# Split weights at shifted addresses in the gate and up stage, and a norm factor spread through DRAM

## The chip, the cores and the metric

The kernel runs on one core of a Trainium2 chip. The metric is the device time of one execution in microseconds. Before the change it was 1467.61 us, the median of three runs (1467.38, 1467.61 and 1486.37 us).

## The reference, cut to what matters

The program is one decoder block on 256 tokens of width 2048, in float32. Two token mixers run on the normed input, an attention and a gated DeltaNet; their outputs are raised to width 2048, gated and added. Then come the output projection and the feed-forward part, which the change touches:

```python
x = x + mixed @ w_o[l]
h2 = rms_norm(x, norm2_w[l])
x = x + (jax.nn.silu(h2 @ w_ffn_gate[l]) * (h2 @ w_ffn_up[l])) @ w_ffn_down[l]
return rms_norm(x, norm_f_w)
```

`rms_norm` multiplies each token's row by one factor, 1/sqrt(mean of squares + eps), and by a weight for each column. The hidden width of the feed-forward part, `D_FF`, is 5632.

## The kernel before, in words

**Matmuls in three parts.** The weights come from DRAM as float32 in pieces of 128 x 2048 words (1 MB, `load`, L134, issued by SP). Each half of a piece is split into a rounded high part `hi` (ScalarE, L159) and the rest `lo` (VectorE, L160), by `split`. There are three `hi` and three `lo` buffers of 1024 words a partition, used in turn. The activations are kept in the same two parts, and a product is three matmuls: high by high, high by low, low by high.

**Two forms of matmul loop.** `group_t` (L234) holds the split weights still: a block of 128 x 128 of `hi` or `lo` is loaded into TensorE, and 256 columns of the activations stream through it. One call makes 256 output features for all tokens. A half of a piece gives 24 such matmuls (16 from `hi`, 8 from `lo`), a call with two pieces 96. `group` and `pair` (through `nat_mm`, L260 to L262) do it the other way: 128 x 128 of the activations stand still, and 512, 354 or 356 columns of the split weights stream.

**Stages in order of time.** The first projection (three blocks 354 and 356 wide, "zab") runs from the start; then `wdn`, `nsa` and `wmg`, 36 calls of `group_t` with the activations `hh`, one `group` ("nsav") between them, and the mixers' own small matmuls put in between by `pump`, which after each half of a piece advances generators that were queued with `add`. Then 16 short calls for `wud` and `wun` (activations `odn` and `onsa`), 48 matmuls each; four `group` calls for `wo` with activations `xa`; 44 calls for gate and up with activations `h2` (named `h` in the profile); and four `group` calls for `wd` with activations `fa` and `fxy`.

**Gate and up.** The loop runs over 22 groups `g`; each makes a gate call and an up call, 192 matmuls together, 4224 in all. After the gate call VectorE multiplies by the factor of norm 2 (`R2b`, L1244), ScalarE takes SiLU (L1245), GpSimd multiplies by the factor again (L1246); after the up call VectorE multiplies the two (L1248) and the product is split into `fa`.

**The factor of norm 2.** VectorE makes two numbers per partition, `r2` (L1213, and `rsqrt`, L275 to L279). Every partition needs all 256 of them in a row: `row_bcast` (L1062) multiplies with the identity on TensorE, once for each half of the tokens, and VectorE copies the result out (L1066). The generator `bcast2` puts the two matmuls after the third and the fourth half of the first gate call.

**The kick.** Before `wud`, a generator `kick` (L965) puts four transposes of the identity, whose result nobody reads, after the first half.

**What sets the order.** Tile's scheduler places instructions per engine in program order, with `split` raised in priority, so that the splits run ahead of their matmuls. Instructions under `pin` keep their order.

**Addresses.** As the program is laid out, the `hi` buffers begin at bytes 41088, 45184 and 49280 of each partition, the `lo` buffers at 53376, 57472 and 61568, the activations `hh` at 78144, `odn` at 127552, `onsa` at 111168, `h2` at 177728, and `xa` and the first `fa` at 78208. The blocks inside them step by 512 or 1024 bytes. So in all `group_t` calls the standing operand begins 64 bytes after the streaming one, counted modulo 256. In `nsav` the same difference is 192, in `wo` it is 0, and so it is in `wd`.

Of the kernel before, what the change touches and what calls it, by code (L numbers as in the profile page):

```python
# [7 lines left out]
F32 = mybir.dt.float32  # L8
F32R = mybir.dt.float32r
# [5 lines left out]
P = 128  # L15
# [3 lines left out]
DFF = 5632  # L19
NFG = DFF // 512  # L20
EPS = 1e-6
ZW = 4288

XW = (4144, 4112, ZW)
NEG = -1e30
# [70 lines left out]
class Kern:  # L96
# [40 lines left out]
    def split_one(self, rv, w, h, ahead):  # L137

        nc = self.nc
        hi = self.wp.tile([P, 1024], F32R, tag="hi", bufs=self.NH, name=self.nm("hi"))  # L140
        lo = self.wp.tile([P, 1024], F32R, tag="lo", bufs=self.NH, name=self.nm("lo"))
        hv = hi[:, :2 * w].rearrange("p (k n) -> p k n", n=w)
        lv = lo[:, :2 * w].rearrange("p (k n) -> p k n", n=w)
        with self.tc.high_priority(offset=self.HP):
            for k in range(2):
                self.pin(nc.scalar.activation(hv[:, k, :], rv[:, 2 * h + k, :], AF.Copy))  # L146
                ahead(2 * h + k)
                self.pin(nc.vector.tensor_tensor(lv[:, k, :], rv[:, 2 * h + k, :], hv[:, k, :].bitcast(F32), op=OP.subtract))
        return hv, lv

    def split(self, rv, w, h):
        nc = self.nc
        m = rv.shape[1] // 2
        hi = self.wp.tile([P, 1024], F32R, tag="hi", bufs=self.NH, name=self.nm("hi"))
        lo = self.wp.tile([P, 1024], F32R, tag="lo", bufs=self.NH, name=self.nm("lo"))
        hv = hi[:, :m * w].rearrange("p (k n) -> p k n", n=w)
        lv = lo[:, :m * w].rearrange("p (k n) -> p k n", n=w)
        with self.tc.high_priority(offset=self.HP):
            nc.scalar.activation(hv, rv[:, m * h:m * h + m, :], AF.Copy)  # L159
            nc.vector.tensor_tensor(lv, rv[:, m * h:m * h + m, :], hv.bitcast(F32), op=OP.subtract)  # L160
        return hv, lv
# [244 lines left out]
    def prep_k(self, pre, cT, hg):  # L406
# [15 lines left out]

        V.tensor_scalar(ss[:], ss[:], EPS, None, op0=OP.add)
        rk = self.rsqrt(ss[:], [2, 4], "rk")
# [99 lines left out]
    def prep_q(self, pre, cT, hg):  # L524
# [5 lines left out]
        for t in range(2):  # L530
# [7 lines left out]
            sq.free()  # L538
        V.tensor_scalar(ss[:], ss[:], EPS, None, op0=OP.add)
        rq = self.rsqrt(ss[:], [2, 4], "rq")  # L540
# [135 lines left out]
    def dn_norm(self, o, t, hg):  # L676
# [9 lines left out]
        V.scalar_tensor_tensor(ss[:], ss[:], 1.0 / 128, cq, op0=OP.mult, op1=OP.mult)  # L686
        V.tensor_scalar(ss[:], ss[:], EPS, None, op0=OP.add)
        r = self.rsqrt(ss[:], [4], "ro")
# [35 lines left out]
    def nsa_kv(self):  # L724
# [3 lines left out]

        while not self.ar.idle("z", ZW):
            yield  # L730
        self.ar.drop("z", ZW)
        zt = self.xy.tile([P, ZW], F32R, tag="z", name="zkh")
        KH = zt[:, 0:2176].rearrange("p (k n) -> p k n", k=2)
# [224 lines left out]
        for v in self.vn:  # L958
            v.free()

    def kick(self):

        bv = self.v4(self.aux("kick"))
        for j in range(4):
            self.pin(self.nc.tensor.transpose(bv[:, j, :], self.cs["ident"], self.cs["ident"]))  # L965
        yield


    def build(self):
        ctx, tc, nc, t = self.ctx, self.tc, self.nc, self.t  # L970
        V = nc.vector
        self.NH = 3
        self.HP = 600
        self.wp = ctx.enter_context(tc.tile_pool(name="wp", bufs=3))
        self.cp = ctx.enter_context(tc.tile_pool(name="cp", bufs=1))
# [32 lines left out]
        self.ar.add("y", ys, 4096)  # L1008
        zs_ = self.xy.tile([P, ZW], F32, tag="z", name="zsg")
        ws_ = self.xy.tile([P, 4096], F32, tag="w", name="wsg")  # L1010
        self.ar.add("z", zs_, ZW)
        self.ar.add("w", ws_, 4096)
# [39 lines left out]
        def norm_factor(ss, name):  # L1052
            v = self.small([2], name + "v")
            V.tensor_scalar(v[:], ss, 1.0 / D, EPS, op0=OP.mult, op1=OP.add)
            r = self.rsqrt(v[:], [2], name)
            return r

        def row_bcast(r, name, steps=1):

            bank = self.aux(name)  # L1060
            for tt in range(2):
                self.pin(nc.tensor.matmul(bank[:, tt * P:(tt + 1) * P], r[:, tt:tt + 1].to_broadcast([P, P]), self.cs["ident"], start=True, stop=True))  # L1062
                if tt == 0 and steps == 2:
                    yield
            R = self.cp.tile([P, 256], F32, name=name)
            V.tensor_copy(R[:], bank[:, :256])  # L1066
            return R
# [5 lines left out]
        rstd1 = self.small([2], "rstd1")  # L1073

        def evac_zab(g, ps):
            w = ZAB_W[g]
            o = 40 if g == 0 else 0
            z0 = sum(ZAB_W[:g]) + o - 40
            for tt in range(2):
                if g == 0:  # L1080
                    V.tensor_scalar(ab[:, tt, :], ps[tt][:, 0:16], rstd1[:, tt:tt + 1], None, op0=OP.mult)
                    V.tensor_scalar(self.gat[:, tt, :], ps[tt][:, 16:40], rstd1[:, tt:tt + 1], None, op0=OP.mult)
                nc.scalar.activation(self.zs[:, tt, z0:z0 + w - o], ps[tt][:, o:w], AF.Silu, scale=rstd1[:, tt:tt + 1])
# [19 lines left out]
        def rms1(ps):  # L1103
            ss = self.small([2], "ssx1")
            V.tensor_reduce(ss[:], ssx[:], axis=AX.X, op=OP.add)
            v = norm_factor(ss[:], "r1")
            V.tensor_copy(rstd1[:], v[:])
            xT.free()
            xn.free()
            evac_zab(0, ps[0])  # L1110
            yield
            evac_zab(1, ps[1])
            yield
            self.R = yield from row_bcast(rstd1, "R1")
            yield from self.dn_small(ab)

        zab = [[t[f"zab{g}"][c] for c in range(4)] for g in range(3)]
        self.add(rows_in())
        ps = self.pair(zab[:2], hact, ZAB_W, first)
        self.add(rms1(ps))  # L1120
        ps = self.group(zab[2], hact, ZAB_W[2])
        evac_zab(2, ps)
# [36 lines left out]
        for g in range(16):  # L1159
            e = self.group_t([t["wmg"][g * 2 + c] for c in range(2)], hact)  # L1160
            m = self.ar.alloc([2, 256])
# [4 lines left out]

        dact = lambda k: self.odn[:, :, k, :]
        nact = lambda k: self.onsa[:, :, k, :]
        self.add(self.kick())
        for g in range(8):  # L1170
            for m in (mg[g], mg[8 + g]):
                self.pin(nc.scalar.activation(m.ap, m.ap, AF.Sigmoid))
# [4 lines left out]
        for g in range(8):  # L1177
            e = self.group_t([t["wun"][g]], nact)
            m = mg[8 + g]
# [18 lines left out]
        for g in range(4):  # L1198
            ps = self.group([t["wo"][g * 4 + c] for c in range(4)], mact)
            cs = slice(g * 512, g * 512 + 512)  # L1200
            for tt in range(2):
# [4 lines left out]
                bv = self.v4(bank)  # L1206
# [6 lines left out]
        V.tensor_reduce(sst[:], ss2[:], axis=AX.X, op=OP.add)  # L1213
        r2 = norm_factor(sst[:], "r2")

        def bcast2():
            for _ in range(2):
                yield
            R2 = yield from row_bcast(r2, "R2", 2)
            self.R2b = R2[:, None, :].to_broadcast([P, 2, 256])  # L1220

        self.add(bcast2())
        h2 = lambda k: hh[k // 4][:, :, k % 4, :]


        fa = []
        for g in range(2 * NFG):
            i = g // 2
            if g % 2 == 0:
                if i < 4:  # L1230
                    if i == 0:
                        fh = self.four(self.hp, "a", "fa", 16, 16)
                    f = fh[i]
                elif i < 10:
                    if i % 2 == 0:
                        j = i // 2 - 2
                        xyt = self.xy.tile([P, XW[j]], F32R, tag="xyz"[j], name=f"fxy{i}")[:, 16 * (j == 1):][:, :4096].rearrange("p (a k n) -> p a k n", a=4, k=4)
                    f = xyt[:, i % 2 * 2:i % 2 * 2 + 2]
                else:
                    f = pb.tile([P, 2064], F32R, name=f"fa{i}")[:, 16:].rearrange("p (l k n) -> p l k n", l=2, k=4)  # L1240
                fa.append(f)
            e = self.group_t([t["wfg"][g * 4 + c] for c in range(2)], h2)
            sgt = pb.tile([P, 2, 256], F32, tag="tmp", bufs=4, name=self.nm("sgt"))
            V.tensor_tensor(sgt[:], e, self.R2b, op=OP.mult)  # L1244
            nc.scalar.activation(sgt[:], sgt[:], AF.Silu)  # L1245
            nc.gpsimd.tensor_tensor(sgt[:], sgt[:], self.R2b, op=OP.mult)  # L1246
            e = self.group_t([t["wfg"][g * 4 + 2 + c] for c in range(2)], h2)
            V.tensor_tensor(sgt[:], e, sgt[:], op=OP.mult)  # L1248
            self.hilo(fa[i][:, :, g % 2 * 2:g % 2 * 2 + 2, :], sgt[:])
        fact = lambda k: fa[k // 4][:, :, k % 4, :]  # L1250
        w_ = pb.tile([P, 4 * 2048 + 48], F32, tag="h2", name="wf")[:, 0:D]
        nc.scalar.dma_start(w_, t["wf"])
# [15 lines left out]
        for g in range(4):  # L1268
# [4 lines left out]
            for tt in range(2):  # L1273
# [8 lines left out]
                if g == 3:  # L1282

                    root = self.small([1], f"root{tt}")
                    nc.scalar.activation(root[:], part, AF.Sqrt, bias=sv)
                V.tensor_scalar(sv, part, sv if g else EPS, None, op0=OP.add)
                if g < 3:
# [110 lines left out]
```

## Time and profile before

| | before |
|---|---|
| median of three runs | 1467.61 us |
| the profiled execution's own time | 1468.2 us |
| its span | 1466.4 us |
| TensorE busy with matmuls | 1453.2 us, 99% |
| VectorE busy | 901.9 us, 62% |
| ScalarE busy | 687.7 us, 47% |
| GpSimd busy | 78.9 us, 5% |
| mean granted clock of TensorE | 0.998 |

The span runs from the first to the last instruction; the profiled execution's own time is 1.8 us more. A matmul's duration in the profile overlaps the next one's, so the pace of a row of matmuls is read from the starts of its first and last, or from a stretch's length and the number of matmuls in it. A stretch's count takes in a matmul that began before it and still ran.

### The profile page before, as it was taken

To read this page: it belongs to the slowest core of one execution; us is meant where nothing else is said; L and a number is where in the kernel's file an instruction comes from. 1 tells how busy PE (TensorE), PEld (TensorE's weight loads), DVE (VectorE), ACT (ScalarE), POOL (GpSimd) and SP (SyncE) were. 2 spreads that over 40 slices of the span, in tenths; PEclk is the share of its full clock that TensorE was granted. 3 is DMA by queue.
4 is the path that set the end of the run, shared out by engine and by line. 5 is a ranking of instruction groups with operands and counts; after the bars stand their busy time and mean duration, and the time that the engine had idled before them with its cause. 6 is when DMAs were issued, how large, how long until landed. Compare 5 with 4: busy or idle time off the path is not lost.

```text
span 1466.4 us, 26003 instructions
## 1 busy us (share of the span) xinstructions
PE 1453.2 (99%) x11021; PEld 1387.7 (95%) x11021; DVE 901.9 (62%) x1352; ACT 687.7 (47%) x850; POOL 78.9 (5%) x69
## 2 busy tenths in 40 slices
PE   9999999999999999999999999999999999999997
PEld 8999999999999999998899999999999998888886
DVE  6678998667687755566565555555555554545454
ACT  5655444354455545444454444444444444444343
POOL 1000101000000000120000000000000000000000
PEclk9999999999999999999999999999999999999999
DMA  8754546435554455555555555555555556555553
GB/s 334 244 201 173 176 162 223 138 129 198 202 198 151 139 204 183 185 180 195 177 197 189 189 198 201 183 194 199 200 187 190 200 198 208 197 200 185 192 198 115
DMA packets 41541, 279.20 MB, mean 190 GB/s; under 512 B 5056, under 2 KB 5584, under 8 KB 9552
## 3 DMA queue, kind: packets, MB, share of 16 engines
q1 hardware_dynamic: 38880, 270.08, 52.7%
q10 hardware_dynamic: 1440, 4.82, 0.9%
q0 software_dynamic: 1104, 2.64, 0.6%
q8 instruction: 86, 1.41, 0.4%
q14 instruction: 31, 0.25, 0.0%
HBM read 274.62 MB, written 2.89 MB: 189 GB/s over the span
## 4 chain that ended last, share of the span: by engine, by line
PE 97%; DMA 1%; DVE 1%; ACT 0%; issue 0%; SPq 0%; DVEq 0%; ACTq 0%
PE mm L234 65%; PE mm L261 9%; PE mm L262 9%; PE mm L260 9%; DMA raw<-in_zab 1%; PE oacc L919 1%; PE U L589 1%; DVE lo L160 0%; PE pt L905 0%; PE hid L772 0%; PE x1T L1208 0%; PE hid L773 0%; ACT hi L159 0%; PE o L606 0%; PE vn L606 0%; PE P L573 0%
## 5 line engine op out<-in xcount | busy, mean ns | idle before, releaser
L160 DVE TENSOR_TENSOR lo<-raw,hi 128x1024 fp32r<-128x1024 f32 (+2 forms) x510 | 617.4, 1212 | 430.5 <-ACT hi L159 429.7
L159 ACT ACTIVATE hi<-raw 128x1024 fp32r<-128x1024 f32 (+2 forms) x510 | 533.6, 1049 | 639.3 <-PE mm L234 388.0
L234 PE MATMUL mm<-h,hi 128*128 128x256 f32 x2816 | 348.7, 277 | 0.0
L234 PEld LDWEIGHTS mm<-h,hi 128*128 128x128 f32 x2816 | 332.5, 188 | 0.1
L234 PE MATMUL mm<-hh,hi 128*128 128x256 f32 x2304 | 291.9, 280 | 1.1 <-ACT hi L159 1.1
L234 PEld LDWEIGHTS mm<-hh,hi 128*128 128x128 f32 x2304 | 275.4, 188 | 1.8 <-ACT hi L159 1.5
L234 PE MATMUL mm<-h,lo 128*128 128x256 f32 x1408 | 188.4, 276 | 0.0
L234 PEld LDWEIGHTS mm<-h,lo 128*128 128x128 f32 x1408 | 172.6, 188 | 0.0
L234 PE MATMUL mm<-hh,lo 128*128 128x256 f32 x1152 | 155.6, 278 | 0.0
L234 PEld LDWEIGHTS mm<-hh,lo 128*128 128x128 f32 x1152 | 142.5, 188 | 0.0
L260 PE MATMUL mm<-hi,fxy 128*128 128x512 f32 x192 | 74.8, 389 | 0.0
L261 PE MATMUL mm<-lo,fxy 128*128 128x512 f32 x192 | 74.8, 389 | 0.0
L262 PE MATMUL mm<-hi,fxy 128*128 128x512 f32 x192 | 74.8, 389 | 0.0
L262 PE MATMUL mm<-hi,fa 128*128 128x512 f32 x160 | 62.3, 389 | 0.0
L260 PE MATMUL mm<-hi,fa 128*128 128x512 f32 x160 | 62.3, 389 | 0.0
L261 PE MATMUL mm<-lo,fa 128*128 128x512 f32 x160 | 62.3, 389 | 0.0
L1246 POOL TENSOR_TENSOR sgt<-sgt,R 128x512 f32<-128x512 f32 x22 | 33.7, 1533 | 531.4 <-ACT sgt L1245 531.4
L261 PE MATMUL mm<-lo,xa 128*128 128x512 f32 x128 | 50.2, 392 | 0.0
L262 PE MATMUL mm<-hi,xa 128*128 128x512 f32 x128 | 50.2, 392 | 0.0
L260 PE MATMUL mm<-hi,xa 128*128 128x512 f32 x128 | 49.9, 390 | 0.0
L261 PE MATMUL mm<-lo,hh 128*128 128x354 f32 (+2 forms) x128 | 44.7, 349 | 0.8 <-DVE lo L160 0.7
L260 PE MATMUL mm<-hi,hh 128*128 128x354 f32 (+2 forms) x128 | 44.0, 350 | 1.2 <-ACT hi L146 0.9
(340 smaller groups left out, 1358.6 us busy)
## 6 DMA issues: line engine op xcount, KB each, us to landing
raw<-in_wfg SPq DMA_DIRECT2D x88, 1024.0 KB, 4.8
raw<-in_wd SPq DMA_DIRECT2D x44, 1024.0 KB, 4.8
raw<-in_wmg SPq DMA_DIRECT2D x32, 1024.0 KB, 4.8
raw<-in_wdn SPq DMA_DIRECT2D x24, 1024.0 KB, 4.8
raw<-in_nsa SPq DMA_DIRECT2D x16, 1024.0 KB, 4.8
raw<-in_wo SPq DMA_DIRECT2D x16, 1024.0 KB, 4.7
raw<-in_wud SPq DMA_DIRECT2D x8, 1024.0 KB, 4.7
raw<-in_wun SPq DMA_DIRECT2D x8, 1024.0 KB, 4.7
```

Of the source, the lines that this page charges most:

```text
L159: nc.scalar.activation(hv, rv[:, m * h:m * h + m, :], AF.Copy)
L160: nc.vector.tensor_tensor(lv, rv[:, m * h:m * h + m, :], hv.bitcast(F32), op=OP.subtract)
L234: nc.tensor.matmul(ps[:, f], (hv, hv, lv)[p][:, k, f * P:f * P + P], a[:, p % 2, :], start=c + h + p + k == 0, stop=c == n - 1 and h + p + ...
L260: nc.tensor.matmul(o, a[:, 0, sl], hv[:, k, :], start=begin, stop=False)
L261: nc.tensor.matmul(o, a[:, 0, sl], lv[:, k, :], start=False, stop=False)
L262: nc.tensor.matmul(o, a[:, 1, sl], hv[:, k, :], start=False, stop=last)
L589: nc.tensor.matmul(bv[:, j, :], Pm[t, hg][:, j, :], U[t, hg][:, j, :], start=True, stop=True)
L919: nc.tensor.matmul(ov[:, j, :], self.vn[kb][:, c:c + 128], pt[:, br * nb + kb, :], start=j == 0 and br == 0 and kb == 0, stop=False, skip_ ...
L1246: nc.gpsimd.tensor_tensor(sgt[:], sgt[:], self.R2b, op=OP.mult)
```

## The change

Four things are done. The `hi` and `lo` buffers grow from 1024 to 1088 words, so that they lie 4352 bytes apart (`hi` at 41088, 45440 and 49792, `lo` at 54144, 58496 and 62848), and all that is allocated after them moves up by 1536 bytes. In groups of odd `g`, the split weights start 4 to 60 words into their buffers, by a table of eleven values; groups of even `g` are not shifted. The factor of norm 2 is written to DRAM by GpSimd's DMA queue and read back to all partitions by a second DMA, in place of the two matmuls and the copy. The kick is taken out.

```diff
+SHIFT = (8, 16, 24, 32, 40, 48, 56, 4, 12, 60, 52)
...
     def split(self, rv, w, h):
         nc = self.nc
         m = rv.shape[1] // 2
-        hi = self.wp.tile([P, 1024], F32R, tag="hi", bufs=self.NH, name=self.nm("hi"))
-        lo = self.wp.tile([P, 1024], F32R, tag="lo", bufs=self.NH, name=self.nm("lo"))
-        hv = hi[:, :m * w].rearrange("p (k n) -> p k n", n=w)
-        lv = lo[:, :m * w].rearrange("p (k n) -> p k n", n=w)
+        hi = self.wp.tile([P, 1088], F32R, tag="hi", bufs=self.NH, name=self.nm("hi"))
+        lo = self.wp.tile([P, 1088], F32R, tag="lo", bufs=self.NH, name=self.nm("lo"))
+        o = self.shift
+        hv = hi[:, o:o + m * w].rearrange("p (k n) -> p k n", n=w)
+        lv = lo[:, o:o + m * w].rearrange("p (k n) -> p k n", n=w)
...
-        self.add(self.kick())
...
-        def bcast2():
-            for _ in range(2):
-                yield
-            R2 = yield from row_bcast(r2, "R2", 2)
-            self.R2b = R2[:, None, :].to_broadcast([P, 2, 256])
-
-        self.add(bcast2())
+        scrR = self.dram.tile([2, 128], F32, name="scrR")
+        R2 = self.cp.tile([P, 256], F32, name="R2")
+        self.pin(nc.gpsimd.dma_start(scrR[:].rearrange("t p -> p t"), r2[:]))
+        self.pin(nc.gpsimd.dma_start(R2[:].rearrange("p (t n) -> p t n", t=2), scrR[:].unsqueeze(0).to_broadcast([P, 2, 128])))
+        self.R2b = R2[:, None, :].to_broadcast([P, 2, 256])
...
+            self.shift = SHIFT[g // 2] if g % 2 else 0
             e = self.group_t([t["wfg"][g * 4 + c] for c in range(2)], h2)
...
+        self.shift = 0
```

The order on the engines changes at three places alone. On TensorE, the first gate call stood before like this (a row is a run of matmuls, `R` is the factor's spread, `h` the activations `h2`):

```order
L234 MATMUL mm_8177<-h_7514,hi_8238 128x256 x16
L234 MATMUL mm_8177<-h_7514,lo_8239 128x256 x8
L1062 MATMUL R_8266<-consts,r_y_8164 128x128
L234 MATMUL mm_8177<-h_7514,hi_8268 128x256 x16
L234 MATMUL mm_8177<-h_7514,lo_8269 128x256 x8
L1062 MATMUL R_8266<-consts,r_y_8164 128x128
L234 MATMUL mm_8303<-h_7514,hi_8306 128x256 x16
L234 MATMUL mm_8303<-h_7514,lo_8307 128x256 x8
```

With the change the same place reads (lines after the table have moved by three):

```order
L237 MATMUL mm_8176<-h_7509,hi_8237 128x256 x16
L237 MATMUL mm_8176<-h_7509,lo_8238 128x256 x8
L237 MATMUL mm_8176<-h_7509,hi_8265 128x256 x16
L237 MATMUL mm_8176<-h_7509,lo_8266 128x256 x8
L237 MATMUL mm_8297<-h_7509,hi_8300 128x256 x16
L237 MATMUL mm_8297<-h_7509,lo_8301 128x256 x8
```

Nothing stands between the matmuls of gate and up any more; the row of the kick is gone in the same way. On GpSimd, the place behind the last additions of `wun` read before:

```order
L1181 TENSOR_TENSOR main<-main 128x512 x7
L1246 TENSOR_TENSOR sgt_8299<-sgt_8299,R_8297 128x512
L1246 TENSOR_TENSOR sgt_8540<-sgt_8540,R_8297 128x512
```

and reads now:

```order
L1175 TENSOR_TENSOR main<-main 128x512 x7
L1213 DMA scrR<-r_y_8159 128x2x1
L1214 DMA R_8172<-scrR 128x256
L1241 TENSOR_TENSOR sgt_8293<-sgt_8293,R_8172 128x512
L1241 TENSOR_TENSOR sgt_8534<-sgt_8534,R_8172 128x512
```

The two DMAs are new. On VectorE the copy (L1066) goes, and the first multiplication by the factor stays between the same two `lo` splits; ScalarE and SP keep their order.

## Rows read from the trace of the kernel before

**Rows 1.** Page, parts 1, 2 and 4: busy time, slices of the span, chain.
```profile
PE 1453.2 (99%) x11021; PEld 1387.7 (95%) x11021; DVE 901.9 (62%) x1352; ACT 687.7 (47%) x850; POOL 78.9 (5%) x69
PEclk9999999999999999999999999999999999999999
...
PE 97%; DMA 1%; DVE 1%; ACT 0%; issue 0%; SPq 0%; DVEq 0%; ACTq 0%
```

**Rows 2.** Stretches, TensorE: us, busy (instructions), granted clock, DMA share, GB/s.
```profile
177.00:190.00 13.00, 13.00 (x117) 1.00 0.61 217
560.00:645.00 85.00, 85.00 (x724) 1.00 0.52 179
760.00:1215.00 455.00, 455.00 (x4017) 1.00 0.56 194
1240.00:1450.00 210.00, 210.00 (x928) 1.00 0.53 186
```

**Rows 3.** Page, part 5, gate and up, then earlier calls: count | busy, mean ns.
```profile
L234 PE MATMUL mm<-h,hi 128*128 128x256 f32 x2816 | 348.7, 277 | 0.0
...
L234 PE MATMUL mm<-hh,hi 128*128 128x256 f32 x2304 | 291.9, 280 | 1.1 <-ACT hi L159 1.1
```

**Rows 4.** Timeline of TensorE at the kick: start us, us, engine, line, names, count.
```profile
556.20 2.05 PE L234 MATMUL mm<-odn,hi 128*128 128x256 f32 x16
558.09 1.11 PE L234 MATMUL mm<-odn,lo 128*128 128x256 f32 x8
559.03 0.60 PE L965 MATMUL kick<-consts 128*128 128x128 f32 x4
559.39 1.78 PE L234 MATMUL mm<-odn,hi 128*128 128x256 f32 x13
```

**Rows 5.** Timeline of TensorE around the spread of norm 2's factor.
```profile
745.60 1.07 PE L234 MATMUL mm<-h,lo 128*128 128x256 f32 x8
746.84 0.46 PE L1062 MATMUL R<-consts,r_y 128*128 128x128 f32 x2 [0.17 <-DVE r_y L279]
747.05 2.13 PE L234 MATMUL mm<-h,hi 128*128 128x256 f32 x16
749.02 1.10 PE L234 MATMUL mm<-h,lo 128*128 128x256 f32 x8
749.96 0.38 PE L1062 MATMUL R<-consts,r_y 128*128 128x128 f32 x2
750.10 2.08 PE L234 MATMUL mm<-h,hi 128*128 128x256 f32 x16
...
752.91 1.98 PE L234 MATMUL mm<-h,hi 128*128 128x256 f32 x16
754.73 1.07 PE L234 MATMUL mm<-h,lo 128*128 128x256 f32 x8
755.63 1.64 PE L234 MATMUL mm<-h,hi 128*128 128x256 f32 x13
```

**Rows 6.** Timeline of TensorE, first and last of nsav's first 36 matmuls, and the next.
```profile
247.17 0.39 PE L260 MATMUL mm<-hi,hh 128*128 128x512 f32 x1
...
255.18 0.39 PE L262 MATMUL mm<-hi,hh 128*128 128x512 f32 x1
255.41 1.83 PE L573 MATMUL P<-wsg,main 128*128 128x128 f32 x15
```

**Rows 7.** Timeline of TensorE, eight matmuls whose weights are read with a stride.
```profile
361.61 0.29 PE L772 MATMUL hid<-hi,zkh 128*68 128x256 f32 x1
...
362.58 0.40 PE L234 MATMUL mm<-hh,hi 128*128 128x256 f32 x2
```

**Rows 8.** Timelines of VectorE and ScalarE around the first use of the factor.
```profile
746.53 0.16 DVE L279 SCALAR_TENSOR_TENSOR r_y<-r_u,r_y 128x2 f32<-128x2 f32 x1
...
751.45 0.42 DVE L1066 COPY R<-R 128x256 f32<-128x256 f32 x1
751.90 0.69 DVE L1244 TENSOR_TENSOR sgt<-mm,R 128x512 f32<-128x512 f32 x1
753.30 1.22 DVE L160 TENSOR_TENSOR lo<-raw,hi 128x1024 fp32r<-128x1024 f32 x1 [0.71 <-ACT hi L159]
...
754.58 0.63 ACT L1245 ACTIVATE sgt<-sgt 128x512 f32<-128x512 f32 x1
755.12 1.04 ACT L159 ACTIVATE hi<-raw 128x1024 fp32r<-128x1024 f32 x1
```

**Rows 9.** Timeline of GpSimd: a small write to DRAM, then spread from there.
```profile
60.62 0.69 POOL L340 DMA_DIRECT2D scrG<-main  x1 [41.98 <-DVE main L338]
64.04 2.19 POOL L357 DMA_DIRECT2D main<-scrG  x4 [2.73 <-DMA scrG<-main]
```

**Rows 10.** DMA issues of GpSimd: count, KB each, median us to landing.
```profile
main<-scrG POOLq DMA_DIRECT2D x4, 256.0 KB, 4.5
...
wsg<-scrTT POOLq DMA_DIRECT2D x4, 64.0 KB, 5.8
```

**Rows 11.** Timeline of TensorE where the second call's first piece is used.
```profile
758.36 1.98 PE L234 MATMUL mm<-h,hi 128*128 128x256 f32 x16
760.17 1.07 PE L234 MATMUL mm<-h,lo 128*128 128x256 f32 x8
761.08 0.62 PE L234 MATMUL mm<-h,hi 128*128 128x256 f32 x4
```

More of the change, by code (lines that the diff above doesn't have):

```diff
@@ L153, in split @@
         m = rv.shape[1] // 2
-        hi = self.wp.tile([P, 1024], F32R, tag="hi", bufs=self.NH, name=self.nm("hi"))
-        lo = self.wp.tile([P, 1024], F32R, tag="lo", bufs=self.NH, name=self.nm("lo"))
-        hv = hi[:, :m * w].rearrange("p (k n) -> p k n", n=w)
-        lv = lo[:, :m * w].rearrange("p (k n) -> p k n", n=w)
+        hi = self.wp.tile([P, 1088], F32R, tag="hi", bufs=self.NH, name=self.nm("hi"))
+        lo = self.wp.tile([P, 1088], F32R, tag="lo", bufs=self.NH, name=self.nm("lo"))
+        o = self.shift
+        hv = hi[:, o:o + m * w].rearrange("p (k n) -> p k n", n=w)
+        lv = lo[:, o:o + m * w].rearrange("p (k n) -> p k n", n=w)
         with self.tc.high_priority(offset=self.HP):
@@ L959, in nsa_q @@
             v.free()
[L961 to L965, printed above, removed]
-        yield
     def build(self):
@@ L1056, in norm_factor, with row_bcast @@
             return r
-        def row_bcast(r, name, steps=1):
+        def row_bcast(r, name):
             bank = self.aux(name)
@@ L1062, in row_bcast @@
                 self.pin(nc.tensor.matmul(bank[:, tt * P:(tt + 1) * P], r[:, tt:tt + 1].to_broadcast([P, P]), self.cs["ident"], start=True, stop=True))
-                if tt == 0 and steps == 2:
-                    yield
             R = self.cp.tile([P, 256], F32, name=name)
@@ L1113, in rms1 @@
             yield
-            self.R = yield from row_bcast(rstd1, "R1")
+            self.R = row_bcast(rstd1, "R1")
             yield from self.dn_small(ab)
@@ L1214, in build @@
         r2 = norm_factor(sst[:], "r2")
-        def bcast2():
-            for _ in range(2):
-                yield
-            R2 = yield from row_bcast(r2, "R2", 2)
-            self.R2b = R2[:, None, :].to_broadcast([P, 2, 256])
-        self.add(bcast2())
+        scrR = self.dram.tile([2, 128], F32, name="scrR")
[3 more added lines that the diff above has]
+        self.R2b = R2[:, None, :].to_broadcast([P, 2, 256])
         h2 = lambda k: hh[k // 4][:, :, k % 4, :]
@@ L1249, in build @@
             self.hilo(fa[i][:, :, g % 2 * 2:g % 2 * 2 + 2, :], sgt[:])
+        self.shift = 0
         fact = lambda k: fa[k // 4][:, :, k % 4, :]
```

## Prediction

> **What bounds the kernel now.** I read the page first: TensorE is busy 99% of the span at full granted clock, and the chain of waits runs over it for 97% [rows 1]. So the time is the number of matmuls times the pace at which they follow each other; work of the other engines counts only where TensorE waits for it. Then I measured that pace by stretches. In gate and up, 4017 matmuls stand in 455.00 us; a matmul lasts 0.28 us and one that began earlier is counted, so the pace is 455.28 / 4017 = 113.3 ns. In wud and wun the same line with the same shapes needs 85.28 / 724 = 117.8 ns [rows 2]. Both are even for the whole stretch, at the same granted clock, with TensorE never idle. The reader is to see two paces of one instruction, 4.45 ns apart.
>
> What tells them apart is not the address alone. In all calls of `group_t` the weights start 64 bytes behind the activations, modulo 256. Within a stretch the weights step by 512 and 1024 bytes and from buffer to buffer, and the pace does not notice; so I count differences modulo 256. With `hh` the pace is 13.28 / 117 = 113.5 ns in one stretch [rows 2], yet its calls' matmuls last 280 ns in the mean against 277 for gate and up [rows 3]: they run at both paces. So at 64 bytes either pace holds itself, and foreign matmuls in between decide which. Gate and up are the largest stage on this edge, 4224 matmuls; 4224 x 4.45 ns = 18.8 us, and the third time shown, 1486.37 us, lies 18.8 us above the median. I take that run as one whose gate and up ran at the slow pace throughout; its trace isn't here.
>
> The streaming of 512 columns shows that the difference matters. In wd, where it is 0, the pace is 210.39 / 928 = 226.7 ns [rows 2], 17/16 of 512 columns at 2.4 GHz; 113.3 ns is the same 17/16 of 256. In nsav, where it is 192, 36 matmuls take 255.41 - 247.17 = 8.24 us, 228.9 ns each [rows 6]. So 0 is fast, 192 slow, 64 either.
>
> **The change part by part.**
>
> *The kick goes.* Its four transposes hold the stream from 559.03 to 559.39 us [rows 4], and about 0.1 us is lost on the matmul behind such a break. -0.45 us. The 24 matmuls ahead of it run at (559.03 - 556.20) / 24 = 117.9 ns, the same slow pace as behind it. So the kick neither caused nor cured that pace, and I count nothing for wud and wun. If they became fast it would be 768 x 4.45 ns = -3.4 us.
>
> *The two matmuls of the spread go.* From 745.60 to 752.91 us there are 56 matmuls, two breaks and a wait for `r2` [rows 5]: 7.31 us. At the fast pace 56 take 6.35 us, as the undisturbed 24 from 752.91 to 755.63 bear out (2.72 us). -0.96 us. VectorE's copy of 0.42 us goes too, beside other work.
>
> *The two DMAs come.* `r2` is ready at 746.53 + 0.16 = 746.7 us [rows 8]. The nearest pair is a small write to DRAM and its spread: 64.04 - 60.62 = 3.4 us from one issue to the next [rows 9], and 4.5 us to landing [rows 10]. So `R2` is there at about 754.6 us, and VectorE's first multiplication begins then instead of at 751.90. Behind it in VectorE's queue stands the next `lo` split (1.22 us, at 753.30 now), which would begin at 755.3; TensorE needs it at 760.17 [rows 8, 11], or 1.0 us earlier without the breaks. ScalarE's SiLU waits too, and behind it the `hi` split that ran from 755.12 for 1.04 us; it would end near 755.3 + 0.63 + 1.04 = 757.0, up to 1.3 us later if the table load slips as well, and is needed at 761.08 - 1.0 = 760.1. The cover is 1.8 us; I take 0. At the dearest row, 5.8 us to landing for each DMA [rows 10] with 0.7 us of issue each, `R2` comes at 759.7, 5.1 us later, and TensorE would wait 3.3 us. On GpSimd's queue only the multiplication by the same factor stands behind.
>
> *The buffers grow.* Modulo 256 no unshifted difference changes, since 4352 and 1536 are multiples of it. Modulo 512 every other buffer changes, but `hh` (320 modulo 512) and `h2` (64) both show 113 ns [rows 2]. I take 0. The bounds are the 3456 earlier calls' matmuls all fast, some 3 ns x 2304 = -6.9 us [rows 3], or all slow, 3456 x 4.45 = +15.4 us.
>
> *The shift.* It touches 11 groups, 2112 matmuls. The difference becomes 64 + 4 x shift: in order 96, 128, 160, 192, 224, 0, 32, 80, 112, 48 and 16. No row shows 256 columns at any of these. From below the price is 0: gate and up already run at 17/16, and no long stretch of either form goes under it. From above: the eight matmuls whose weights are read with a stride take (362.58 - 361.61) / 8 = 121 ns [rows 7], 8.0 ns over; on all 4224 that is 33.7 us. I go by the nearest row. 160 and 192 lie by the slow 192; 0 and 16 by the fast 0; 80, 96, 112 and 48 by 64, where a pace is kept; 128, 224 and 32 lie between two. So two shifted groups turn slow, and of 128 and 224 I count one: three. A group without shift keeps the pace it inherits, so the slow pace goes on in the three after them, until the shift of 48 words (difference 0). Six groups of 192 at 4.45 ns: +5.1 us.
>
> **Sum.** 1468.2 (the profiled execution's own time) - 0.45 - 0.96 + 5.1 = 1471.9 us. The median of the runs shown is 0.6 us lower, so I say 1471 us.
>
> **The rivals.**
> - *Offsets mean nothing to TensorE.* What speaks for it: one address difference shows both paces, so the pace may be pure history; gate and up, now without any break, would then stay fast. Against it: nsav against wd [rows 2, 6]. Time: 1467.6 - 1.4 = 1466 us. The Trainium skill, page "SBUF — State Buffer", section "Who interferes with whom", says just this: TensorE has two independent read ports, one for the streaming operand and one for the weights' loading, and never waits on anyone; by that rule the shift costs nothing. The two paces at equal clock don't agree with it, unless something else than reads makes them. If wud and wun turned fast as well, 1463 us.
> - *The slow pace takes the stage.* Most of the shifts turn it slow, or the stream enters slow from the last transposes of `wo`, and nothing breaks the stage any more: before, two breaks gave it a second and third draw. For it: the run of 1486.37 us. Against it: 0 held the fast pace for 928 matmuls, and this difference is among the shifts. Time: 1466 + 12 to 19, about 1482 us.
> - *Slower for good.* A shifted load is as dear as the strided one, and the unshifted groups between don't recover. At 8.0 ns on 4224 matmuls: 1466 + 33.7 = 1500 us. It decides from (29.4 + 1.4) / 4224 = 7.3 ns for each matmul of the stage, or 14.6 if the shifted ones pay alone; the first is 0.7 below the dearest row, the second above all.
> - *The factor comes late.* 3.3 us on top of the forecast, 1475 us.
>
> **How the numbers follow.** Forecast 45% (its own range 1467 to 1477), offsets mean nothing 24% and with wud and wun fast another 8%, slow pace in the stage 15%, late factor 4%, slower for good 4%. The range of 1463 to 1483 us leaves out the case of 1500, about half of the slow-stage case and part of the one at 1463: some 15 to 20 in 100. A change of 2%, 29 us, is about what a measurement of this kernel can tell from none. Only the case of 1500 goes beyond, and part of it stays within: slower 0.03. For faster, the stage would have to fall to 113.3 - (29.4 - 1.4) / 4.224 = 106.7 ns a matmul, under the 17/16 that no long stretch undercuts: 0.01.
>
> **What would show it.** In the trace after: gaps of L1062 and the kick gone; VectorE's first multiplication by `R2` at some 754 us with TensorE never idle there; and above all the pace of each group of gate and up. Right is 113.3 ns in most, 117.8 in about six, beginning near shifts of 16 to 32 words and ending at 48. An even 113.3 ns would show that shifts don't matter to a stream that runs fast, and paces other than these two would make both the classes and the sum wrong.

## The result, and the profile after

The changed kernel takes 1485.17 us (median of 14 runs, 1484.56 to 1485.88), the kernel before 1468.39 us beside it. The ratio is 1.0105, with a 95% interval of 1.0087 to 1.0124: 1% slower, within the 2% that count as the same, and outside the range of 1463 to 1483 us. Of the fourteen runs of the kernel before, thirteen lie between 1467.1 and 1471.0 us and one at 1486.4; those of the changed kernel lie within 1.3 us of each other. The profiled execution took 1485.14 us, its span is 1483.4 us, 17.0 more than before.

The page of the changed kernel, parts 1, 4 and 5, beside [rows 1, 3] (L237 is L234 of before, L162 and L163 are the splits):

```profile
PE 1466.4 (99%) x11013; PEld 1400.6 (94%) x11013; DVE 901.7 (61%) x1351; ACT 687.2 (46%) x850; POOL 80.3 (5%) x71
...
PE 87%; issue 8%; DMA 2%; DVE 1%; POOL 1%; ACT 1%; SPq 0%; ACTq 0%; DVEq 0%; POOLq 0%
...
L237 PE MATMUL mm<-h,hi 128*128 128x256 f32 x2816 | 357.7, 280 | 0.0
...
L237 PE MATMUL mm<-hh,hi 128*128 128x256 f32 x2304 | 292.1, 279 | 1.1 <-ACT hi L162 1.1
L237 PE MATMUL mm<-h,lo 128*128 128x256 f32 x1408 | 192.3, 279 | 3.8 <-DVE lo L163 3.8
```

TensorE's busy time grew by 13.2 us and the matmuls of gate and up from 277 to 280 ns; those of the earlier calls did not slow down. A wait of 3.8 us for a `lo` split is new. The chain now leads back over the factor's two DMAs to GpSimd, and most of its 8% "issue" is the time that GpSimd stood idle before the first of them: the factor arrives late.

The stretches of TensorE in gate and up show which groups pay. Columns are as in [rows 2]; each stretch lies within one group of 192 matmuls, and the pace is its length plus 0.28 us, divided by the count, good to some 0.6 ns. In order the rows are shifted by 8 words, not, 16, not, 24, 32, 40, 48, not, 56, not, 4, 12, 60 and 52 words; the unshifted groups not shown read like the second row.

```profile
769.10:788.00 18.90, 18.90 (x163) 1.00 0.58 211
789.00:809.00 20.00, 20.00 (x179) 1.00 0.59 206
811.00:832.00 21.00, 21.00 (x179) 1.00 0.53 195
834.00:854.00 20.00, 20.00 (x179) 1.00 0.54 202
856.00:877.00 21.00, 21.00 (x177) 1.00 0.53 191
900.00:921.00 21.00, 21.00 (x188) 1.00 0.57 197
944.00:965.00 21.00, 21.00 (x183) 1.00 0.54 193
988.00:1010.00 22.00, 22.00 (x186) 1.00 0.52 185
1011.00:1032.00 21.00, 21.00 (x180) 1.00 0.53 193
1034.00:1055.00 21.00, 21.00 (x180) 1.00 0.53 190
1057.00:1077.00 20.00, 20.00 (x172) 1.00 0.55 194
1079.00:1100.00 21.00, 21.00 (x179) 1.00 0.55 195
1124.00:1145.00 21.00, 21.00 (x177) 1.00 0.54 193
1169.00:1189.00 20.00, 20.00 (x173) 1.00 0.55 197
1213.00:1234.00 21.00, 21.00 (x180) 1.00 0.54 193
```

Taken from the starts of a group's 192 matmuls (for 8 words from its second call alone, since the first stands behind the wait), the paces are:

| shift, words | 8 | 16 | 24 | 32 | 40 | 48 | 56 | 4 | 12 | 60 | 52 |
|---|---|---|---|---|---|---|---|---|---|---|---|
| difference modulo 256, bytes | 96 | 128 | 160 | 192 | 224 | 0 | 32 | 80 | 112 | 48 | 16 |
| pace, ns | 117.3 | 118.6 | 120.0 | 113.3 | 116.7 | 120.0 | 118.3 | 118.7 | 120.0 | 117.8 | 118.4 |

Ten of eleven shifted groups are slow; only 32 words is not. The unshifted groups run at 113.3 ns, but for the two that follow the shifts of 48 and 56 words, at 117.8. Added up over 113.3 ns, the shifted groups pay 10.1 us and these two unshifted ones 1.7.

The rest is the factor. Timelines of TensorE, GpSimd and VectorE in the changed kernel, and its DMA issues (as in [rows 10]):

```profile
757.85 1.98 PE L237 MATMUL mm<-h,hi 128*128 128x256 f32 x16
763.67 1.25 PE L237 MATMUL mm<-h,lo 128*128 128x256 f32 x8 [3.85 <-DVE lo L163]
764.72 3.56 PE L237 MATMUL mm<-h,hi 128*128 128x256 f32 x16
768.12 1.10 PE L237 MATMUL mm<-h,lo 128*128 128x256 f32 x8
...
747.45 0.75 POOL L1213 DMA_DIRECT2D scrR<-r_y  x1 [101.71 <-DVE r_y L282]
756.62 0.59 POOL L1214 DMA_DIRECT2D R<-scrR  x1 [8.42 <-DMA scrR<-r_y]
...
750.08 1.22 DVE L163 TENSOR_TENSOR lo<-raw,hi 128x1024 fp32r<-128x1024 f32 x1 [1.44 <-ACT hi L162]
761.79 0.69 DVE L1239 TENSOR_TENSOR sgt<-mm,R 128x512 f32<-128x512 f32 x1 [10.49 <-DMA R<-scrR]
...
R<-scrR POOLq DMA_DIRECT2D x1, 128.0 KB, 5.2
...
scrR<-r_y POOLq DMA_DIRECT2D x1, 1.0 KB, 8.9
```

The write of 1 KB takes 8.9 us to land, the read 5.2; VectorE stands from 751.3 to 761.8 us, and TensorE runs out of `lo` splits for 3.85 us. The eight matmuls behind the wait still start 131 ns apart; the run of 16 after them takes 764.72 to 768.12 us, 213 ns each. The second row of these stretches tells why (the first is wud and wun without the kick, 83.28 / 707 = 117.8 ns):

```profile
562.00:645.00 83.00, 83.00 (x707) 1.00 0.53 181
764.90:767.90 3.00, 3.00 (x16) 0.50 0.79 322
```

The granted clock was 0.50, 1.2 GHz, behind 3.85 us without matmuls. The 48 matmuls from 757.85 us on take 11.2 us, where 24 at 113.3 and 24 at 117.3 ns would take 5.5: wait and slow clock together are 5.7 us.

**The account.** Shifted groups 10.1, the two unshifted ones 1.7, late factor 5.7, the two breaks gone -1.0: +16.5 us, which is what gate and up grew by. The span grew by 17.0. The other 0.5 us lie ahead: wud began at 557.16 us in place of 556.20, and wud and wun, without the kick, took 0.44 less. The first of these is scatter, as the traces of the kernels below show: in all but one, which changes the earlier calls, wud begins between 555.4 and 558.0.

### The profile page after: what moved, and what is told of

It is laid out like the page before. It is cut to its first block, busy times and chain, and to the rows that moved or that the text cites. A ratio compares the mean times of both kernels' runs of the same rounds, so it can differ in the third digit from the quotient of the medians.

```text
span 1483.4 us, 25990 instructions
## 1 busy us (share of the span) xinstructions
PE 1466.4 (99%) x11013; PEld 1400.6 (94%) x11013; DVE 901.7 (61%) x1351; ACT 687.2 (46%) x850; POOL 80.3 (5%) x71
## 4 chain that ended last, share of the span: by engine, by line
PE 87%; issue 8%; DMA 2%; DVE 1%; POOL 1%; ACT 1%; SPq 0%; ACTq 0%; DVEq 0%; POOLq 0%
PE mm L237 62%; PE mm L264 7%; PE mm L265 6%; PE mm L263 6%; DMA raw<-in_zab 1%; POOL main L1175 1%; DVE lo L163 1%; PE oacc L922 1%; PE U L592 1%; ACT hi L162 1%; PE pt L908 0%; DMA R<-scrR 0%; DVE main L1174 0%; PE hid L775 0%; PE hid L776 0%
## 5 line engine op out<-in xcount | busy, mean ns | idle before, releaser
L163 DVE TENSOR_TENSOR lo<-raw,hi 128x1024 fp32r<-128x1024 f32 (+2 forms) x510 | 617.8, 1213 | 435.1 <-ACT hi L162 434.2
L162 ACT ACTIVATE hi<-raw 128x1024 fp32r<-128x1024 f32 (+2 forms) x510 | 533.1, 1048 | 646.2 <-PE mm L237 395.5
L237 PE MATMUL mm<-h,hi 128*128 128x256 f32 x2816 | 357.7, 280 | 0.0
L237 PEld LDWEIGHTS mm<-h,hi 128*128 128x128 f32 x2816 | 341.5, 189 | 0.1
L237 PE MATMUL mm<-hh,hi 128*128 128x256 f32 x2304 | 292.1, 279 | 1.1 <-ACT hi L162 1.1
L237 PEld LDWEIGHTS mm<-hh,hi 128*128 128x128 f32 x2304 | 275.5, 188 | 1.9 <-ACT hi L162 1.5
L237 PE MATMUL mm<-h,lo 128*128 128x256 f32 x1408 | 192.3, 279 | 3.8 <-DVE lo L163 3.8
L237 PEld LDWEIGHTS mm<-h,lo 128*128 128x128 f32 x1408 | 176.4, 188 | 4.0 <-DVE lo L163 4.0
L237 PE MATMUL mm<-hh,lo 128*128 128x256 f32 x1152 | 155.7, 277 | 0.0
L237 PEld LDWEIGHTS mm<-hh,lo 128*128 128x128 f32 x1152 | 142.6, 188 | 0.0
```

Source lines behind the costliest of these rows:

```text
L237: nc.tensor.matmul(ps[:, f], (hv, hv, lv)[p][:, k, f * P:f * P + P], a[:, p % 2, :], start=c + h + p + k == 0, stop=c == n - 1 and h + p + ...
```

## The experiments

**The shifts alone.** The kernel before, with the buffers and the table of the change; factor on TensorE, kick in place.

```diff
         self.add(bcast2())
...
+            self.shift = SHIFT[g // 2] if g % 2 else 0
             e = self.group_t([t["wfg"][g * 4 + c] for c in range(2)], h2)
```

> The kernel before with the larger buffers and the change's table of shifts; norm 2's factor stays on TensorE, the kick stays. If the shifts cost what the trace of the change shows (10.2 us in the shifted groups and 1.7 us in the groups after the shifts of 48 and 56 words), it takes 1468.4 + 11.9 = 1480 us, with the same paces group by group as in the changed kernel: 117.3, 118.6, 120.0, 113.3, 116.7, 120.0, 118.3, 118.6, 120.0, 117.8 and 118.4 ns. If the paces hang on history (which breaks stood before), they differ from these. If the late factor is what made the change slow, the time is near 1468 us.

Measured: 1480.65 us, 1.0063 of before (1.0030 to 1.0097). The paces repeat to 0.1 ns but for the first: 120.0 ns at 8 words, where the changed kernel had 117.3. Four stretches, for 8, 24, 32 and 48 words:

```profile
764.00:784.00 20.00, 20.00 (x169) 1.00 0.55 196
...
853.00:874.00 21.00, 21.00 (x177) 1.00 0.54 190
897.00:918.00 21.00, 21.00 (x188) 1.00 0.54 198
...
985.00:1007.00 22.00, 22.00 (x185) 1.00 0.52 187
```

The unshifted groups repeat too, with 117.8 ns behind 48 and 56 words alone. So the shifts cost 12 us by themselves, and but for 8 words the paces follow the table, not the factor's path.

**The factor through DRAM alone.** The changed kernel with every shift at zero.

```diff
-            self.shift = SHIFT[g // 2] if g % 2 else 0
+            self.shift = 0
```

> The changed kernel with all shifts at zero: factor through DRAM, no kick, larger buffers. If the factor's lateness costs what the trace of the change shows (a wait of 4.0 us and 16 matmuls at half the clock, 1.6 us), it takes 1468.4 - 1.4 + 5.6 = 1472.6 us, with gate and up at 113.3 ns behind the wait, or at 117.8 ns if the wait chose the slow pace: then 1490 us. If the lateness was a consequence of the shifts, about 1467 us.

Measured: ten runs at 1472.3 to 1473.4 us (five) and 1488.7 to 1493.6 us (four), and a single one of 3832.6 us that nothing here explains; ratio 1.0059 (1.0000 to 1.0118). The profiled execution, 1472.83 us, has the wait again, and runs at 113.3 ns behind it:

```profile
761.88 2.08 PE L237 MATMUL mm<-h,lo 128*128 128x256 f32 x8 [3.75 <-DVE lo L163]
763.75 3.62 PE L237 MATMUL mm<-h,hi 128*128 128x256 f32 x16
...
762.00:766.00 4.00, 4.00 (x19) 0.50 0.75 264
790.00:1200.00 410.00, 410.00 (x3620) 1.00 0.55 194
```

Here the clock stood at 0.50 from the first matmul behind the wait on, 234 ns each, so the slow clock cost 2.9 us and not 1.7. The first cluster is near the 1472.6 expected for the wait. The second is 15 to 21 us above; 4000 matmuls at the slow pace would add 17.8. A wait that ends at a moment that varies may draw the pace anew, but that is not shown: no trace of a run in that cluster was taken, and the kernel before has single runs at 1487 us without a wait.

**One constant offset.** The kernel before with all gate and up weights shifted by 48 words; then the same with the activations `h2` moved up by 48 words as well. (The second also moves the last `fa` tile, so that 96 matmuls of wd stand at a difference of 192.)

```diff
+            self.shift = 48
             e = self.group_t([t["wfg"][g * 4 + c] for c in range(2)], h2)
```
```diff
-        hh = self.four(pb, "h2", "h2", 48, 48)
+        hh = self.four(pb, "h2", "h2", 96, 96)
```

> The kernel before with larger buffers and one constant shift of 48 words in all 44 calls of gate and up, so that the weights start 0 bytes after the activations, modulo 256. If the pace is set by the weights' address (their own, or its difference to the activations), all 4224 matmuls run at the 120.0 ns that the change showed at this shift: 1468.4 + 28.2 = 1496.6 us. If it is the change of the offset from call to call that costs, there is none here: 1468 us, or 1487 us at an even 117.8 ns.

> As the constant shift of 48 words, with the activations of gate and up moved up by 48 words too, so that the difference is 64 bytes again. If the difference between weights and activations sets the pace: 113.3 ns, 1468.4 us (or an even 117.8 ns and 1487 us, since both paces occur at this difference). If the weights' own address does: 120.0 ns, 1496.6 us.

Measured: the first takes 1495.96 us in four runs, 1.0166 of before (1.0106 to 1.0225), 0.6 off the expectation. The second has runs of 1468.1 to 1469.2 us (four) and 1486.5 to 1489.2 us (six), ratio 1.0054 (1.0000 to 1.0108); its profiled run took 1468.36 us. One stretch of each, first 0, then 64 bytes, and in the second kernel the first of wd's matmuls at 192 and the first behind them:

```profile
790.00:1200.00 410.00, 410.00 (x3419) 1.00 0.53 183
...
790.00:1190.00 400.00, 400.00 (x3531) 1.00 0.55 194
...
1272.40 0.39 PE L261 MATMUL mm<-hi,fa 128*128 128x512 f32 x1
...
1277.89 0.39 PE L261 MATMUL mm<-hi,fa 128*128 128x512 f32 x1
```

410.28 / 3419 = 120.0 ns and 400.28 / 3531 = 113.4 ns. The weights lie at the same addresses in both kernels, and the activations of the first lie, modulo 256, as in the kernel before, which has 113.3 ns. So neither address alone sets the pace but the two together, as their difference does, and no change of offset from call to call is needed. At a difference of 64 either cluster comes out. In wd the 24 matmuls at 192 take 5.49 us, 229 ns each, and those around them, at 0, 226.7: with 512 columns 192 is the slow one, as nsav's rows had it.

**All calls at 192.** Weights of every `group_t` call shifted by 32 words, the one shift that cost nothing.

```diff
-                hv, lv = self.split(rv, 256, h)
+                hv, lv = self.split(rv, 256, h, 32)
```

> The kernel before with all weights of group_t shifted by a constant 32 words, so that the difference is 192 in every call of wdn, nsa, wmg, wud, wun, gate and up (8448 matmuls). The change ran 192 matmuls at this difference, at 113.3 ns. If 192 has the fast pace alone, all stages run at 113.3 ns: wud and wun give 3.4 us, the earlier calls some 4 us, 1468.8 - 7.5 = 1461 us, and no run is at 1487 us. If 192 keeps either pace as 64 does (both differ from 0 by half of 128), the stages mix as before: 1468 us, single runs at 1487 us. If it was fast in the change only by what stood before it, 1487 us or more.

Measured: ten runs at 1473.0 to 1474.0 us and one, the profiled, at 1491.72 us; ratio 1.0004 (0.9961 to 1.0047). Its stretches in wmg, in wud and wun, and in gate and up:

```profile
400.50:418.00 17.50, 17.50 (x157) 1.00 0.52 181
562.00:645.00 83.00, 83.00 (x707) 1.00 0.53 184
790.00:1200.00 410.00, 410.00 (x3483) 1.00 0.53 187
```

113.3, 117.8 and 117.8 ns. So 192 keeps either pace, as 64 does. It isn't better: in this trace wud begins at 561.22 us, 5.0 later than before, since more of the earlier calls' matmuls ran slow, and the ten runs are 5 us longer than those near 1468.

**A detour as a reset.** The kernel with weights and activations moved, its first up call shifted by 4 words more.

```diff
             e = self.group_t([t["wfg"][g * 4 + c] for c in range(2)], h2)
...
+            self.shift = 48 + 4 * (g == 0)
             e = self.group_t([t["wfg"][g * 4 + 2 + c] for c in range(2)], h2)
```

> The kernel with weights and activations of gate and up moved by 48 words (its runs took 1468 or 1487 us, 4 and 6 of 10), but with the first up call, 96 matmuls, shifted by 4 words more: difference 80, then 64 again for the 42 calls that follow. In both traces with the change's table, 64 was fast behind 80, also where 64 had been slow ahead of it. If the pace of an unshifted call is set by the offset of the call before, every run is fast: 1468.4 + 96 x 5.4 ns = 1469 us. If chance at the breaks sets it, 1469 and 1487 us again.

Measured: four runs, 1486.13 to 1487.34 us; ratio 1.0105 (1.0043 to 1.0167). The stretch behind the detour:

```profile
790.00:1200.00 410.00, 410.00 (x3483) 1.00 0.54 188
```

117.8 ns in all 42 calls. In the changed kernel the calls behind the same offset ran at 113.3. So the offset of the call before doesn't decide the pace by itself; this theory of mine fell.

**The factor written as it lies.** No shifts, no kick; the factor goes to DRAM as 128 rows of 8 bytes, comes back as one row of 1 KB, and VectorE puts it in order. The buffers are back at 1024 words, here and in the kernels after it, so this kernel differs from the one with the factor through DRAM alone in that too; the differences modulo 256 stay.

```diff
-        scrR = self.dram.tile([2, 128], F32, name="scrR")
+        scrR = self.dram.tile([128, 2], F32, name="scrR")
...
+        Rr = self.cp.tile([P, 256], F32, name="Rr")
+        self.pin(nc.gpsimd.dma_start(scrR[:], r2[:]))
+        self.pin(nc.gpsimd.dma_start(Rr[:].rearrange("p (n t) -> p n t", t=2), scrR[:].unsqueeze(0).to_broadcast([P, 128, 2])))
+        V.tensor_copy(R2[:].rearrange("p (t n) -> p t n", t=2), Rr[:].rearrange("p (n t) -> p t n", t=2))
```

> The kernel with the factor through DRAM and no shifts (1472 us where gate and up are fast), with the factor written as it lies, 8 bytes for each partition in one row, in place of 256 words of 4 bytes that are put in another order; read back as one row of 1 KB for each partition, and put in order by a copy on VectorE. If the scattered words make the write slow (8.9 us to landing), it now takes about 3.2 us as the small write of 16 rows does, TensorE no longer waits and keeps its clock: 1472.6 - 5.6 = 1467 us in fast runs. If the write is slow because it stands behind the weights' DMAs, 8.9 us and 1472.6 us stay.

Measured: 1466.91 us, ten runs from 1466.74 to 1467.99; ratio 0.9980 (0.9955 to 1.0006). The two DMAs, and the stretches of wud and wun and of gate and up:

```profile
Rr<-scrR POOLq DMA_DIRECT2D x1, 128.0 KB, 4.2
...
scrR<-r_y POOLq DMA_DIRECT2D x1, 1.0 KB, 4.4
...
562.00:645.00 83.00, 83.00 (x707) 1.00 0.53 185
750.00:1200.00 450.00, 450.00 (x3973) 1.00 0.56 195
```

The write lands in 4.4 us in place of 8.9, so half of that was the scattered words of 4 bytes; the 3.2 us expected were too few. The wait is gone, and with neither break nor wait in gate and up the profiled run has 113.3 ns throughout, and none of the ten lies near 1487 us. wud and wun remain at 117.8 ns.

**A kick of another length.** The last kernel, with a kick of one, two or three transposes after the first half of wud.

```diff
+        for j in range(1):
+            self.pin(self.nc.tensor.transpose(bv[:, j, :], self.cs["ident"], self.cs["ident"]))
```

> The kernel with the factor written as it lies (1466.9 us), with a kick of one transpose in front of the second half of wud in place of none; with four, as before, and with none, wud and wun ran at 117.8 ns. If the break's exact length chooses the pace, one of one, two and three transposes may start the 744 matmuls at 113.3 ns: 1466.9 + 0.2 - 3.3 = 1463.8 us. If something in this stage holds the slow pace (other buffers, other activations), 117.8 ns and 1467.1 us whatever the kick.

> The same with two transposes: 1466.9 + 0.3 - 3.3 = 1463.9 us if they start the fast pace, 1467.2 us with 117.8 ns in wud and wun if the stage holds the slow one.

> The same with three transposes: 1466.9 + 0.4 - 3.3 = 1464.0 us if they start the fast pace, 1467.3 us with 117.8 ns in wud and wun if the stage holds the slow one.

Measured: one transpose 1463.62 us (1463.25 to 1465.65), ratio 0.9950 (0.9911 to 0.9989); two 1467.51 us; three 1467.37 us. wud and wun with one transpose, then with two:

```profile
562.00:640.00 78.00, 78.00 (x691) 1.00 0.54 188
...
562.00:640.00 78.00, 78.00 (x665) 1.00 0.53 187
```

78.28 / 691 = 113.3 ns against 117.7; with three transposes it is 117.8. Same addresses, same shapes: the number of transposes in the break chose, here and not by a rule that I could name. This kernel takes 0.5% less than the one before the change; the interval lies below 1, and within the 2% that count as the same.

## Why the prediction was wrong

**The bound** held: the path is TensorE's pace, and at 64 bytes two paces keep themselves.

**The kick** and the **two breaks**: the terms held, at 0.44 and 1.0 us. Without the kick wud and wun stay at 117.8 ns, in the changed kernel as in the one with the factor written as it lies, and the first gate call runs through.

**The factor** failed: 0 was taken, the bounds ended at 3.3 us, 5.7 came. The pair of rows that I took for it [rows 9] writes 16 rows of 512 bytes; this write is 256 words of 4 bytes, to be put in another order, and no row showed such a one. From one issue to the next it took 9.2 us in place of 3.4. The dearest row, 5.8 us, was of another pattern as well. `r2` was ready at 747.15 us here, and VectorE used the factor 14.6 us later where 7.9 were expected: 6.7 us too late. The wait ended with the `lo` split. By the prediction's own numbers that split would end at 755.3 + 1.2 = 756.5 us and was needed at 759.2, a cover of 2.7 us; 6.7 - 2.7 = 4.0 us is what TensorE's next matmul was late. The 1.8 us that the prediction took were the cover of ScalarE's path, which did not decide. So the path was right, and the time to the write's landing was the term that was mis-sized. That the clock would stand at 0.50 behind the wait, for 1.7 us more, was not in the sum.

**The shift** failed most: 5.1 us was forecast, 11.8 came. The step at fault is "I go by the nearest row". The differences 0 and 192 were classed by rows of 512 streaming columns; with 256 columns they are the other way round, 0 among the slowest at 120.0 ns and 192 as fast as 64 can be. Thus 192 was taken for slow, and six of the classes "near 64, keeps its pace" or "fast" turned out slow. What is fast in 256 columns are 64 and 192. Nor are there only two paces, as the sum assumed: the shifted groups also show 116.7, 118.6 and 120.0 ns, and paces other than the two were the prediction's own sign against its sum. Nor did the slow pace go on behind a slow group as a rule: it did behind 48 and 56 words alone.

**The rivals.** The measured time is near that of the slow-stage rival, 1482 us, but not by its mechanism: ten of the 22 groups ran at 113.3 ns, and 5.7 us were the factor's. "The factor comes late" came true as well, beside the shifts and not in place of them; the prediction priced the two one at a time. "Offsets mean nothing" is refuted by the constant shift, 120.0 against 113.4 ns. The page "SBUF — State Buffer" of the Trainium skill, section "Who interferes with whom", lets TensorE never wait on anyone. The two kernels that differ, for gate and up, in the activations' place alone (120.0 and 113.4 ns) don't agree with it, if it is the reads that cost; no run shows that they are.

**What stays open.** Why a break or a wait starts one pace and not the other. The number of transposes in a kick chose it, and an offset taken for one call did not cure it; what in the timing decides was not found. Neither was why 8 words gave 117.3 ns once and 120.0 once. Only the differences 0, 64 and 192 were held over a whole stage. The others ran for 192 matmuls each, always in the table's order, so what part of their pace is the difference, and what part what stood before, is not separated.

## What to carry to other kernels

Where TensorE is the bound, read the pace of each stretch from the starts of its matmuls, and compare stretches of the same shape: here it went from 113.3 to 120.0 ns at full clock, by nothing but the distance of the two operands in memory and by what stood before. Test an offset by a constant one over a whole stage, in the form that will run, since a row of another width said the opposite. Where a few bytes for every partition go by way of DRAM, try to write them as they lie and order them on chip: here the write's landing fell from 8.9 to 4.4 us, and with it went a wait of TensorE and the half clock behind that.

## What the runs showed of the hardware

- Loading 128 x 128 weights while 256 columns stream: with the start of the weights minus the start of the columns at 0 bytes modulo 256, a matmul took 120.0 ns throughout gate and up; at 64 and 192 it took 113.3 or 117.8 ns, and in gate and up the pace once begun held for some 4000.
- With 512 columns it was the other way round: 226.7 ns at 0, 229 at 192, in one stage of one trace.
- One transpose of 128 x 128 in the stream, in place of none, two, three or four, had 720 of the following 744 matmuls run at 113.3 ns in place of 117.8, with all seven runs of that kernel within 2.4 us.
- The fastest long stretches took 113.3 ns for 256 columns and 226.7 for 512, 17/16 of one column per cycle at 2.4 GHz.
- Around waits of TensorE of 3.85 and 3.75 us the granted clock fell to 0.50, for 3.4 and for 6.8 us; that cost 1.7 and 2.9 us beyond the waits' own length.
- A write of 1 KB to DRAM took 8.9 us to land as 256 reordered words of 4 bytes, and 4.4 as 128 rows of 8 bytes.
